# A decoder layer with two token mixers: where the first chunk of the gated attention is loaded and split

## The chip, the core and the metric

The kernel runs on one core of a Trainium2 chip. The core has TensorE (PE, matmuls), VectorE (DVE), ScalarE (ACT) and GpSimd (POOL) for arithmetic, and SyncE (SP), which here only issues transfers (DMAs) between the chip's main memory and the on-chip memory. ACT issues some transfers too. Each engine takes its instructions in the order in which they are written, and an instruction waits until the semaphores of what it needs have risen. The metric is the device time of one execution in microseconds.

## The reference

One step of a layer with `D_MODEL` = 1024, for a prompt of 2048 tokens and 8 sample tokens:

```
shift, scale, gate = c @ w_c + b_c
h = x * (1 + scale) + shift
z = h @ w_in + b_in        # q, k, v | attn gate | conv GLU in | conv gate | merge gates mA, mB
A: o = dilated sliding-window attention, three groups of heads, weighted by their softmax sums
   a = (o * silu(attn gate)) @ w_pa
B: u = GLU -> causal depthwise conv, width 31 -> LayerNorm -> swish
   b = (u * silu(conv gate)) @ w_pb
y = (sigmoid(mA) * a + sigmoid(mB) * b) @ w_o
x_out = LayerNorm(alpha * x + gate * y)
```

The outputs are `x_out` of prompt and samples, the new keys and values, and the tail of the convolution. All is float32.

## The kernel before, in words

Every large product is made of reduced-precision matmuls: each operand is split into a high part H (a copy rounded by ACT) and a low part L (the rest, subtracted by DVE or POOL), and PE adds up H·H, H·L and L·H. A split is therefore always two instructions, ACT first.

**The product z** (`quad`, L498) takes nearly 1800 us in two passes. Beside it, generators called lanes write the attention, the convolution and the combination of heads into the same instruction streams: `tick` (and, at the end, `run_lanes`) steps the lane that is due by an assumed clock, and a lane's `yield` tells how much later its next step is due. What a lane issues stands behind what was written before on each engine. The last pairs of z are the merge gates; they are evicted by ACT (L698, L705) and stored to `tm_d` and `tn_d` on ACT's queue. The gated attention goes to `og_d` (4 x 128 channels x 2056 tokens), the gated convolution to `cg_d`, both in main memory.

**The output's weights** are 16 pieces of 128 x 1024: pieces 0 to 3 are w_pa (tiles `wc0H`, `wc0L`), 4 to 7 w_pb (`wc1H`, `wc1L`), 8 to 15 w_o (`wc2`, `wc3`). `p_load` loads a piece into an `xr` buffer; there are three of them, in the pool "op". A buffer is taken again when its old content has been read, and the load waits for the last reader. `p_split` (L1439, L1440) splits piece x with ACT and with DVE (odd x below 8) or POOL (the others), and then issues the load of piece x + 3.

**The lane `early_out`**, which opens "op" when the attention is done, loads pieces 0 to 2 and splits pieces 0 to 3 beside the last pairs of z, one step every 4 us of the lanes' clock.

**The output stage** opens the pool "rc" after z. It works through the tokens in eight chunks `cc` of 256. For chunk 0 it loads `og_d` and `cg_d` (`oc_load`, into `ocr`), splits them into `oH`, `oL` and `bH`, `bL` (`oc_split`, L1609, L1610: DVE for oL, POOL for bL), splits pieces 4 to 7, and loads the merge gates (`mrg`). Then PE computes four blocks of a (`pab`, 48 matmuls of oH and oL with `wc0`), four of b (`py`, of bH and bL with `wc1`), and the same for the other four blocks (L1709); DVE weighs and adds them; the product with w_o follows (L1765). Later chunks are loaded and split while the chunk ahead is computed. All these loads are on SP, in this order: pieces 4, 5, 6, `og_d`, `cg_d`, piece 7, pieces 8 to 10, `mrg`.

Of the kernel before, what the change touches and what calls it, by code (L numbers as in the profile page):

```python
# [9 lines left out]
F32R = mybir.dt.float32r  # L10
AF = mybir.ActivationFunctionType
OP = mybir.AluOpType
# [4 lines left out]
P = 128  # L17
D = 1024
L = 2048
# [22 lines left out]
def f32(ap):  # L42
    return ap.bitcast(F32)
# [3 lines left out]
def hybrid_layer(ctx: ExitStack, tc: tile.TileContext, I, O):  # L47
    nc = tc.nc
    ctx.enter_context(tc.manual_schedule())
    PE, ACT, DVE, POOL = nc.tensor, nc.scalar, nc.vector, nc.gpsimd  # L50

    def ld(out, in_):
        nc.sync.dma_start(out, in_)
# [42 lines left out]
    def flush(every=True):  # L96
        fns = [x for x in post if every or x[0] <= clock["pe"]]
        post[:] = [x for x in post if x not in fns]
        for _, fn in fns:
            fn()  # L100
# [33 lines left out]
    og_d = dp.tile([4, P, T], F32, name="og_d")  # L134
# [1284 lines left out]
    pieces = []  # L1419
# [5 lines left out]
    def xbuf():  # L1425
        return op_[0].tile([P, D], F32, name="xr", tag="xr", bufs=3)

    def p_load(x):
        nm, kt, tag, k = pieces[x]
        praw[x] = xbuf()  # L1430
        ld(praw[x], I[nm][kt * P:(kt + 1) * P, :])

    def p_split(x):
        nm, kt, tag, k = pieces[x]
        if k == 0:
            wC[tag] = tuple((op_ if tag == 0 else rc_)[0].tile([P, 4, D], F32R, name=f"wc{tag}{n}") for n in "HL")
        H, Lo = (t[:, k, :] for t in wC[tag])
        r = praw.pop(x)
        ACT.activation(H, r, AF.Copy)  # L1439
        (DVE if k % 2 and x < 8 else POOL).tensor_tensor(Lo, r, f32(H), op=OP.subtract)  # L1440
        if x + 3 < len(pieces):
            p_load(x + 3)

    op_, rc_ = [], []

    def early_out():

        while ("at", 1) not in done:
            yield 1.0
        leave("cv1")  # L1450
        op_.append(enter("op"))
        for x in range(3):
            p_load(x)
        yield 8.0
        for x in range(4):
            p_split(x)
            yield 4.0


    zdone = set()  # L1460
# [17 lines left out]
    def enter(name):  # L1478
        cm, pool = opened(name, bufs=1, side="right")
        open_[name] = cm  # L1480
        return pool

    def leave(name):
        flush()
        closed(open_.pop(name))
# [30 lines left out]
    for p in range(2):  # L1516
        state["p"] = p
        cv = None
        for n, pair in enumerate(quads[p]):
            kind, a, b = pair[0]  # L1520
            ut = None
            if kind == "ua":
                if cv is None:
                    cv = enter(f"cv{p}")
                    if p == 0:
                        at_lane.add(at_first())
                        mix_lane.add(conv_samples(cv))
                        mix_lane.add(norm_samples(cv))
                        mix_lane.add(conv_norm(cv))
                        smp_lane.add(samples())  # L1530
                    else:
                        at_lane.add(at_second())
                        mix_lane.add(conv_norm(cv))
                        mix_lane.add(combine(cv))
                        mix_lane.add(early_out())
                if a >= 2:
                    while ("conv", p, a - 2) not in done:
                        conv_step()
                    if p:
                        guard(("urows", a - 2))  # L1540
                ut = cv.tile([P, 1054], F32, name="u", tag="u", bufs=2)
                if p == 0:
                    POOL.memset(ut[:, 0:30], 0.0)
                else:
                    POOL.tensor_copy(ut[:, 0:30], utail[:, a, :])
                evs = ev_glu(a, col_of(pair[0]), col_of(pair[1]), ut)
            else:
                evs = evs_of(pair)
# [40 lines left out]
    rc = enter("rc")  # L1589
    rc_.append(rc)  # L1590
    psC = ctx.enter_context(tc.tile_pool(name="psC", bufs=4, space=PSUM))
    bH, bL, oH, oL = (rc.tile([P, 4, 264], F32R, name=n) for n in ("bH", "bL", "oH", "oL"))
    yH, yL = (rc.tile([P, 8, 264], F32R, name=n) for n in ("yH", "yL"))
    gate, lng, lnb = (rc.tile([P, D], F32, name=n) for n in ("gate", "lng", "lnb"))

# [5 lines left out]
    def oc_load(cc, z):  # L1601
        t0, n = 256 * cc, 256 if cc < 7 else 264
        r = ocr[z] = rc.tile([P, 4, 264], F32, name="ocr", tag="ocr", bufs=2)
        ld(r[:, :, :n], (og_d, cg_d)[z][:].rearrange("j p t -> p j t")[:, :, t0:t0 + n])

    def oc_split(cc, z):
        n = 256 if cc < 7 else 264
        (H, Lo), r = ((oH, oL), (bH, bL))[z], ocr.pop(z)
        ACT.activation(H[:, :, :n], r[:, :, :n], AF.Copy)  # L1609
        (DVE, POOL)[z].tensor_tensor(Lo[:, :, :n], r[:, :, :n], f32(H[:, :, :n]), op=OP.subtract)  # L1610
# [7 lines left out]
            out.append(t)  # L1618
        return out

    oc_load(0, 0)
    oc_load(0, 1)
    oc_split(0, 0)
    oc_split(0, 1)
    for x in range(4, 8):
        p_split(x)
# [72 lines left out]
    for cc in range(8):  # L1699
        n = 256 if cc < 7 else 264  # L1700
        mgn = []
        for d in range(8):
# [30 lines left out]
            if cc == 0:  # L1733
                p_split(8 + d)
                if d == 7:
                    for t in range(3):
                        xr_load(t)
                    ld(gate, rows_bcast(gate_d[0], P))
                    ld(lng, rows_bcast(I["ln_g"], P))
                    ld(lnb, rows_bcast(I["ln_b"], P))  # L1740
# [84 lines left out]
```

## Time and profile before

| what | value |
|---|---|
| time, median of 3 runs | 2204.65 us (2203.07 to 2206.36) |
| the profiled execution's own time | 2208.26 us |
| its span, first to last instruction | 2206.4 us |
| share of the span busy: PE, DVE, ACT, POOL | 96%, 60%, 42%, 42% |
| mean granted clock of PE | 0.984 |
| last matmul group of z starts | 1795.49 us |
| first matmul of the output stage starts | 1800.73 us |

The profile is of one execution. Rows of a timeline give start, duration, engine, line of the kernel, operation and tiles (out<-in), and in brackets the idle time ahead of it with the instruction that ended it. The chain of waits goes back from the last instruction to what released it at each step. "SPq" and "ACTq" are the issuing of transfers on SP and ACT; "DMA" in the chain is a transfer on its way. Idle time of an engine costs something only where another one waits for it in the end.

### The profile page before, as it was taken

Reading aid. Unit: us, or ns where it says so; the run is one execution under the profiler, and the core shown is the slowest. Engines: PE = TensorE matmul, PEld = TensorE weight load, DVE = VectorE, ACT = ScalarE, POOL = GpSimd, SP = SyncE. Lnnn points to the kernel's source line nnn. Section 1 sums busy time; section 2 is a strip of 40 time slices with the busy share of each in tenths; the row PEclk is TensorE's granted clock in tenths of the full one; section 3 lists DMA queues with packets and bytes.
Section 4 is the critical chain, followed back from the end, with each engine's and each line's share of the span. In section 5 each row is a group of like instructions: output and inputs, shape, how many; then the busy total and the mean of one; then the engine's idle time right before and its main releaser. Section 6 shows DMA issues by size and latency. Waiting matters only on the chain.

```text
span 2206.4 us, 36413 instructions
## 1 busy us (share of the span) xinstructions
PE 2109.8 (96%) x13185; PEld 1864.7 (85%) x13185; DVE 1333.1 (60%) x2121; ACT 918.3 (42%) x2056; POOL 930.2 (42%) x950
## 2 busy tenths in 40 slices
PE   7799999999998899989999999999999988999998
PEld 3799999999998869968888888888878877888886
DVE  4667776777758733444776677634467827555456
ACT  3424444444444535644444444456555533111110
POOL 2455454444634432454444445445323446232332
PEclk9899999999999999989999999999999999999999
DMA  8365455455668765435555556567898866333220
GB/s 262 94 178 185 144 185 160 154 156 185 196 200 275 227 210 175 152 104 148 163 165 161 169 164 190 187 189 234 263 296 262 261 212 223 124 124 106 97 98 31
DMA packets 404046, 392.09 MB, mean 178 GB/s; under 512 B 26585, under 2 KB 331277, under 8 KB 402833
## 3 DMA queue, kind: packets, MB, share of 16 engines
q1 hardware_dynamic: 336277, 342.63, 50.3%
q10 hardware_dynamic: 67588, 47.13, 6.7%
q8 instruction: 104, 1.70, 0.3%
q14 instruction: 77, 0.63, 0.1%
HBM read 245.91 MB, written 144.29 MB: 177 GB/s over the span
## 4 chain that ended last, share of the span: by engine, by line
PE 53%; DVE 4%; DMA 2%; issue 1%; POOL 1%; ACT 1%; ACTq 0%; SPq 0%; POOLq 0%; DVEq 0%
PE ps_Z L498 9%; PE ps_W L498 9%; PE ps_X L498 9%; PE py L1765 8%; PE pab L1709 5%; PE ps_Y L498 4%; PE ps_S L1208 3%; PE ps_U L1248 1%; PE ps_S L1233 1%; DVE yL L76 1%; PE ps_S L653 1%; DVE xr L80 1%; PE ps_U L1246 1%; DVE st L1648 0%; DMA u<-orow 0%
## 5 line engine op out<-in xcount | busy, mean ns | idle before, releaser
L247 POOL TENSOR_TENSOR bop<-raw,bop 128x512 fp32r<-128x512 f32 x341 | 485.8, 1430 | 568.2 <-ACT bop L238 441.3
L498 PE MATMUL ps_W<-As,bop 128*128 128x258 f32 (+1 forms) x2448 | 437.7, 327 | 15.8 <-DVE zst L80 15.8
L498 PEld LDWEIGHTS ps_W<-As,bop 128*128 128x128 f32 x2448 | 360.5, 191 | 57.1 <-DVE zst L80 18.6
L80 DVE SCALAR_TENSOR_TENSOR y<-u,cwT,y 128x1024 f32<-128x1024 f32 x240 | 357.8, 1491 | 1.8
L238 ACT ACTIVATE bop<-raw 128x512 fp32r<-128x512 f32 x409 | 251.5, 624 | 76.8 <-DVE raw L76 26.4
L498 PE MATMUL ps_X<-As,bop 128*128 128x258 f32 (+1 forms) x1224 | 220.3, 327 | 11.3 <-ACT c L568 6.7
L498 PE MATMUL ps_Z<-As,bop 128*128 128x258 f32 (+1 forms) x1224 | 224.6, 330 | 2.4 <-ACT c L568 2.2
L498 PE MATMUL ps_X<-Aa,bop 128*128 128x258 f32 (+1 forms) x1224 | 219.8, 328 | 5.2 <-ACT bop L238 1.6
L498 PE MATMUL ps_Y<-Aa,bop 128*128 128x258 f32 (+1 forms) x1224 | 218.6, 326 | 0.0
L498 PE MATMUL ps_Z<-Aa,bop 128*128 128x258 f32 (+1 forms) x1224 | 217.9, 327 | 0.0
L498 PEld LDWEIGHTS ps_X<-As,bop 128*128 128x128 f32 x1224 | 179.7, 191 | 30.2 <-ACT c L568 6.9
L498 PEld LDWEIGHTS ps_X<-Aa,bop 128*128 128x128 f32 x1224 | 182.0, 192 | 26.5 <-ACT bop L238 2.8
L498 PEld LDWEIGHTS ps_Z<-As,bop 128*128 128x128 f32 x1224 | 180.1, 191 | 22.4 <-ACT c L568 2.6
L498 PEld LDWEIGHTS ps_Z<-Aa,bop 128*128 128x128 f32 x1224 | 181.9, 191 | 18.2 <-issue 0.8
L498 PEld LDWEIGHTS ps_Y<-Aa,bop 128*128 128x128 f32 x1224 | 179.3, 190 | 18.3 <-issue 1.8
L1225 ACT ACTIVATE X<-X,mz 128x128 f32<-128x128 f32 (+1 forms) x192 | 87.0, 455 | 168.3 <-DVE mz L84 162.4
L80 DVE SCALAR_TENSOR_TENSOR zst<-ps_W,bT,c 128x258 f32<-128x258 f32 (+1 forms) x102 | 58.4, 573 | 136.4 <-ACT c L589 133.1
L247 DVE TENSOR_TENSOR bop<-raw,bop 128x512 fp32r<-128x512 f32 x68 | 51.9, 763 | 94.4 <-ACT bop L238 90.9
L80 DVE SCALAR_TENSOR_TENSOR X<-ps_S,tabh 128x512 f32<-128x512 f32 (+1 forms) x80 | 52.5, 656 | 83.0 <-PE ps_S L1208 76.0
L1662 ACT ACTIVATE xr<-xr,lnm 128x1024 f32<-128x1024 f32 (+1 forms) x16 | 19.9, 1244 | 183.7 <-POOL lnm L1661 171.2
L80 DVE SCALAR_TENSOR_TENSOR zst<-ps_Y,bT,c 128x258 f32<-128x258 f32 (+1 forms) x90 | 51.4, 571 | 71.3 <-PE ps_Y L498 48.6
L1208 PE MATMUL ps_S<-ak,aq 128*128 128x256 f32 (+1 forms) x256 | 90.4, 484 | 0.3 <-DMA ak<-zk 0.3
(309 smaller groups left out, 3786.8 us busy)
## 6 DMA issues: line engine op xcount, KB each, us to landing
raw<-w_in SPq DMA_DIRECT2D x205, 256.0 KB
raw<-tw_d SPq DMA_DIRECT2D x136, 256.0 KB
tw_d<-raw SPq DMA_DIRECT2D x102, 256.0 KB
tw_d<-t SPq DMA_DIRECT2D x34, 256.0 KB
rawb<-w_in SPq DMA_DIRECT2D x33, 256.0 KB
wc<-w_c SPq DMA_DIRECT2D x16, 512.0 KB
aq<-zq SPq DMA_DIRECT2D x16, 512.0 KB
xr<-x_prompt SPq DMA_DIRECT2D x16, 512.0 KB
```

The costliest lines, as they stand in the source:

```text
L76: DVE.tensor_tensor(out, a, b, op=op)
L80: DVE.scalar_tensor_tensor(out, a, s, b, op0=op0, op1=op1)
L238: ACT.activation(t[:, 0], r, AF.Copy)
L247: eng.tensor_tensor(t[:, 1], r, f32(t[:, 0]), op=OP.subtract)
L498: PE.matmul(acc[:, :n], w[:, i, b, :], a[:, b, off:off + n], start=start and b == 0 and x == 0, stop=b == 3 and x == 2, skip_group_check=True)
L653: PE.transpose(pt[:, i * P:(i + 1) * P], t[:, i * P:(i + 1) * P], ident)
L1208: PE.matmul(S[:, s:s + w, :], q_of(b), k_of(b, w), start=True, stop=True)
L1225: ACT.activation(X[:, s:s + w, :], X[:, s:s + w, :], AF.Exp, bias=mz[:, n, 0:1], accum_out=mz[:, n, 1:2])
L1233: PE.transpose(pt[:, s, :], X[:, s, :], ident)
L1246: PE.matmul(U[:, n, :], Y[:, s, :], v_of(b, 1), start=True, stop=False)
L1709: PE.matmul(p[:, :n], a, b[:, kt, :n], start=i == 0, stop=i == 11)
L1765: PE.matmul(py[h], a[:, d, c0:c0 + P], w[:, h * 512:(h + 1) * 512], start=f, stop=l)
```

## The change

The lane `early_out` gets a fifth step. After the split of piece 3 it takes `oH` and `oL` from the pool "op" (they were in "rc"), takes an `xr` buffer, loads the first 256 tokens of `og_d` into it, yields 5 us of the lanes' clock, splits it with ACT and POOL, and then issues the load of piece 6, which the split of piece 3 used to issue. The output stage no longer loads and splits `og_d` for chunk 0; the later chunks use the same `oH` and `oL` as before.

```diff
         (DVE if k % 2 and x < 8 else POOL).tensor_tensor(Lo, r, f32(H), op=OP.subtract)
-        if x + 3 < len(pieces):
+        if x + 3 < len(pieces) and x != 3:
             p_load(x + 3)
 
+    oH_ = {}
@@ early_out
         for x in range(4):
             p_split(x)
             yield 4.0
+        flush()
+        for x in "HL":
+            oH_[x] = op_[0].tile([P, 4, 264], F32R, name="o" + x)
+        r = xbuf().rearrange("p (j n) -> p j n", j=4)
+        ld(r, og_d[:].rearrange("j p t -> p j t")[:, :, 0:256])
+        yield 5.0
+        ACT.activation(oH_["H"][:, :, :256], r, AF.Copy)
+        POOL.tensor_tensor(oH_["L"][:, :, :256], r, f32(oH_["H"][:, :, :256]), op=OP.subtract)
+        p_load(6)
@@ output stage
-    bH, bL, oH, oL = (rc.tile([P, 4, 264], F32R, name=n) for n in ("bH", "bL", "oH", "oL"))
+    bH, bL = (rc.tile([P, 4, 264], F32R, name=n) for n in ("bH", "bL"))
+    oH, oL = oH_["H"], oH_["L"]
...
-    oc_load(0, 0)
     oc_load(0, 1)
-    oc_split(0, 0)
     oc_split(0, 1)
```

The order of the instructions shows where this puts them. A row is a line of the kernel, an operation, its tiles (with numbers that tell buffers apart) and the engines or DMA semaphores that it waits for.

On SP, before, from the load of piece 5 to that of the first w_o piece (`xr` are weight pieces):

```order
L53 DMA xr_19243<-w_pb 128x1024 [waits DMAHW6_49,DMAHW5_49,Pool_49]
L53 DMA xr_19266<-w_pb 128x1024 [waits DMAHW7_49,DMAHW3_49,DVE_49]
L53 DMA ocr_19331<-og_d_122 128x4x256 [waits PE_49]
L53 DMA ocr_19333<-cg_d_123 128x4x256 [waits DMAHW4_49]
L53 DMA xr_19343<-w_pb 128x1024 [waits DMAHW5_49,Pool_49]
L53 DMA xr_19347<-w_o 128x1024 [waits DMAHW6_49,DVE_49]
```

Here piece 6 waits for DVE, and the two chunks follow it. In the changed kernel the same stretch of SP reads:

```order
L53 DMA xr_19243<-w_pb 128x1024 [waits DMAHW6_49,DMAHW5_49,Pool_49]
L53 DMA xr_19311<-og_d_122 128x4x256 [waits DMAHW7_49,DMAHW3_49,DVE_49]
L53 DMA xr_19315<-w_pb 128x1024 [waits DMAHW7_49,Pool_49]
L53 DMA ocr_19335<-cg_d_123 128x4x256 [waits DMAHW4_49,PE_49]
L53 DMA xr_19343<-w_pb 128x1024 [waits DMAHW5_49,Pool_49]
L53 DMA xr_19347<-w_o 128x1024 [waits DMAHW6_49,DVE_49]
```

The load of `og_d` stands ahead of piece 6 with the wait that piece 6 had; piece 6 waits for POOL; `cg_d` follows.

On POOL, the splits from piece 2 to piece 6, before:

```order
L1440 TENSOR_TENSOR wc0L_19178<-xr_19112,wc0H_19177 128x1024 [waits DMAHW5_49,Activation_49]
L1610 TENSOR_TENSOR bL_19323<-ocr_19333,bH_19322 128x4x256 [waits DMAHW4_49,Activation_49]
L1440 TENSOR_TENSOR wc1L_19340<-xr_19210,wc1H_19339 128x1024 [waits PE_49,Activation_49]
L1440 TENSOR_TENSOR wc1L_19340<-xr_19266,wc1H_19339 128x1024 [waits DMAHW7_49,Activation_49]
L1440 TENSOR_TENSOR wc2L_19477<-xr_19347,wc2H_19476 128x1024 [waits DMAHW6_49,PE_49,Activation_49]
```

These are piece 2, bL, pieces 4, 6 and 8. In the changed kernel:

```order
L1440 TENSOR_TENSOR wc0L_19178<-xr_19112,wc0H_19177 128x1024 [waits DMAHW5_49,Activation_49]
L1466 TENSOR_TENSOR oL_19310<-xr_19311,oH_19309 128x4x256 [waits DMAHW2_49,DMAHW7_49,DVE_49,Activation_49]
L1621 TENSOR_TENSOR bL_19329<-ocr_19335,bH_19328 128x4x256 [waits DMAHW4_49,Activation_49]
L1440 TENSOR_TENSOR wc1L_19340<-xr_19210,wc1H_19339 128x1024 [waits PE_49,Activation_49]
L1440 TENSOR_TENSOR wc1L_19340<-xr_19315,wc1H_19339 128x1024 [waits DMAHW3_49,Activation_49]
```

oL has come from DVE, ahead of bL.

On ACT of the changed kernel, from the last eviction of z (`zst`) on:

```order
L698 ACTIVATE zst_19306<-ps_Z_19137,hbT_131 128x512 [waits DMAHW2_49,PE_49]
L56 DMA tm_d_124<-zst_19306 128x512 [waits Activation_49]
L1465 ACTIVATE oH_19309<-xr_19311 128x4x256 [waits DMAHW7_49]
L1620 ACTIVATE bH_19328<-ocr_19335 128x4x256 [waits DMAHW4_49,Pool_49]
L1439 ACTIVATE wc1H_19339<-xr_19210 128x1024
L1439 ACTIVATE wc1H_19339<-xr_19243 128x1024 [waits DMAHW6_49]
```

oH has the place that it had before (there L1609, reading `ocr`).

## The prediction

> **What bounds the kernel now.** I read the busy shares first, then the chain of waits around the change (1767 to 1830 us), then the timeline of each engine there.
>
> ```profile
> span 2206.4 us, 36413 instructions
> PE 2109.8 (96%) x13185; PEld 1864.7 (85%) x13185; DVE 1333.1 (60%) x2121; ACT 918.3 (42%) x2056; POOL 930.2 (42%) x950
> ```
>
> TensorE (PE) is busy nearly all the time, so what a change around 1800 us is worth is what it does to the few places where PE stands still. The last product of z and the first product of the output meet there. PE's timeline (start, duration, and in brackets the idle time before and who ended it):
>
> ```profile
> 1795.49 2.95 PE L498 MATMUL ps_Z<-Aa,bop 128*128 128x512 f32 x12
> 1800.73 0.38 PE L1709 MATMUL pab<-oH,wc0H 128*128 128x256 f32 x1 [2.29 <-ACT oH L1609]
> 1801.99 0.45 PE L1709 MATMUL pab<-oL,wc0H 128*128 128x256 f32 x1 [0.88 <-DVE oL L1610]
> ...
> 1809.18 0.28 PE L1709 MATMUL py<-bH,wc1H 128*128 128x256 f32 x1
> ...
> 1812.34 0.56 PE L1709 MATMUL py<-bH,wc1H 128*128 128x256 f32 x1 [1.94 <-ACT wc1H L1439]
> ...
> 1813.60 0.58 PE L1709 MATMUL py<-bH,wc1L 128*128 128x256 f32 x1 [0.48 <-DVE wc1L L1440]
> ```
>
> PE loses about 3 us at oH/oL, then computes the 48 matmuls of `pab` (1801.99 to 1809.18), and stops again in `py` until the split of piece 7, the last of w_pb, is there at 1813.60. Which of the two stops sets the end? The chain of waits (start, duration, what) says the second, and that it hangs on cg_d, not on og_d:
>
> ```profile
> 1789.01 2.89 DVE wc0L L1440
> ...
> 1791.92 0.33 SPq L53
> 1792.25 0.05 issue
> 1792.30 0.43 SPq L53
> 1792.73 0.05 issue
> 1792.78 7.75 DMA ocr<-cg_d
> ...
> 1804.14 3.38 POOL wc1L L1440
> 1807.52 0.02 issue
> 1807.54 3.67 DMA xr<-w_pb
> 1811.21 0.02 issue
> 1811.24 1.06 ACT wc1H L1439
> 1812.30 0.02 issue
> 1812.32 1.24 DVE wc1L L1440
> ```
>
> To be read as: at 1791.9 DVE has split piece 3 and frees its `xr` buffer; SP then issues three loads one behind the other, piece 6 (1791.92), og_d (1792.30) and cg_d (1792.78). cg_d lands at 1792.78 + 7.75 = 1800.53. Then bH and bL are split, then POOL splits piece 4 until 1807.52, which frees the buffer for piece 7; piece 7 lands, is split by ACT and DVE until 1813.56, and PE goes on at 1813.60. From cg_d's landing to PE's restart it is 13.07 us, all of it a chain.
>
> **The change, part by part.** The rows of the order shown with the change carry this part. On SP, og_d has taken the place and the wait of piece 6 (DVE's split of piece 3). Piece 6 now waits for POOL: the three `xr` buffers hold pieces 4 and 5, both unsplit, and og_d, so the only buffer that can come free is og_d's, by POOL's oL. cg_d is queued behind piece 6. On POOL, oL stands ahead of bL. On ACT nothing moved: oH still stands behind the last eviction of z and its store, and the four `wc1H` still stand behind bH, so behind cg_d.
>
> *Step 1, the load of og_d.* Issued at 1791.92 and not 1792.30, and first of its group. That is worth nothing, since oH is held by ACT's own order:
>
> ```profile
> 1798.47 0.69 ACT L698 ACTIVATE zst<-ps_Z,hbT 128x512 f32<-128x512 f32 x1 [1.37 <-PE ps_Z L498]
> 1799.19 0.33 ACTq L56 DMA_DIRECT2D tm_d<-zst  x1
> 1799.62 1.06 ACT L1609 ACTIVATE oH<-ocr 128x1024 fp32r<-128x1024 f32 x1 [0.46 <-ACT zst L698]
> 1800.61 1.06 ACT L1609 ACTIVATE bH<-ocr 128x1024 fp32r<-128x1024 f32 x1
> ```
>
> Before, og_d had already landed when ACT came to it (its idle time was ended by zst, not by a DMA). So oH stays at 1799.62 to 1800.68, and PE's first `pab` matmul at 1800.73.
>
> *Step 2, oL on POOL.* DVE's oL, and on POOL the same shape as bL:
>
> ```profile
> 1800.71 1.23 DVE L1610 TENSOR_TENSOR oL<-ocr,oH 128x1024 fp32r<-128x1024 f32 x1 [4.27 <-ACT oH L1609]
> ...
> 1818.88 0.42 DVE L80 SCALAR_TENSOR_TENSOR ev<-mrg,pab 128x256 f32<-128x256 f32 x1 [5.33 <-DMA mrg<-tm_d]
> ```
>
> ```profile
> 1801.74 2.44 POOL L1610 TENSOR_TENSOR bL<-ocr,bH 128x1024 fp32r<-128x1024 f32 x1 [10.93 <-ACT bH L1609]
> ```
>
> oL ends at 1800.70 + 2.44 = 1803.14, not 1801.94: PE's second `pab` matmul comes 1.2 us later. That lies inside the wait in `py`, so it costs nothing by itself.
>
> *Step 3, piece 6 and cg_d.* Piece 6 is issued when oL is done, 1803.16 with a 0.02 us step, takes 0.33 us of SP, then 0.05 us, and cg_d's issue starts at 1803.54, where it was 1792.78: 10.76 us later. Its time to land is not 7.75 us any more, since fewer transfers are in flight. The nearest row is the first `mrg` load, which has the same size and shape (512 KB, 128x4x256) and also follows a weight piece by one issue:
>
> ```profile
> 1807.98 5.92 SPq L53 DMA_DIRECT2D xr<-w_o  x3
> 1814.00 0.39 SPq L53 DMA_DIRECT2D mrg<-tm_d  x1
> ```
>
> Issued at 1814.00 and awaited by DVE until 1818.88: 4.88 us. Bounds: 3.67 us (piece 7 with nothing ahead of it) and 7.75 us (as before). I take 4.88: cg_d lands at 1803.54 + 4.88 = 1808.42, where it was 1800.53. That is **7.89 us later** (6.7 and 10.8 at the bounds).
>
> *Step 4, what hangs on it.* bH starts with cg_d's landing before (1800.61) and after. Behind it the order on every engine is as it was: four `wc1H` on ACT, bL and pieces 4 and 6 on POOL, pieces 5 and 7 on DVE, piece 7's load behind the split of piece 4. Piece 6 lands before cg_d, so `wc1H` of piece 6 doesn't wait. So the 13.07 us stay, and PE restarts in `py` at 1808.42 + 13.07 = 1821.5. `pab` is over by about 1810.4 and no longer covers anything. A gain here could be that POOL's 3.38 us for piece 4 shrinks to the 2.44 us that bL of the same size took, by 0.9; I see no row that would change beside it, so I take none and keep it for the range.
>
> *Step 5, passing on.* The w_o pieces and the `mrg` loads stand on SP behind piece 7, as before, and all later loads behind these; DVE's 5.33 us of waiting for `mrg` moves along. Nothing behind 1813.6 depends on a clock of its own that could take the shift back. The early rows keep their order; DVE's split of piece 1 has a changed set of waits (now POOL in it). If that is POOL's split of piece 0, it may cost it 0.2 us around 1783.4, which ends well ahead of piece 3's split and changes nothing.
>
> The sum against the profiled execution: 0 + 0 + 7.9 + 0, so span 2206.4 + 7.9 = 2214.3 and its own time 2208.26 + 7.9 = 2216.2. That execution is 3.6 us above the median of the runs, 2204.65; the same shift on the median gives **2212.5 us**.
>
> **Weighing the clock.** The granted clock (the last three columns are clock, DMA share, GB/s) around the restart of `py`:
>
> ```profile
> 1814.00:1816.00 2.00, 2.00 (x11) 2.00 (x11) 0.00 (x0) 0.00 (x0) 0.00 (x0) 0.50 0.58 162
> ...
> 1820.00:1822.00 2.00, 2.00 (x19) 1.96 (x17) 1.14 (x3) 0.74 (x2) 0.00 (x0) 1.00 1.08 355
> ```
>
> After stops of 1.94 and 0.48 us PE already runs at half clock, 11 matmuls in 2 us against 19 later. So the kernel before pays the slow restart, and a longer stop adds nothing. [...]
>
> **Rivals.**
> - *A, the wait is not the new oL.* If piece 6's wait on POOL is long fulfilled, SP issues it and cg_d right behind og_d, and cg_d lands near 1800.5. Then only POOL's order costs: bL ends 1803.14 + 2.44 = 1805.58 instead of 1804.18, 1.4 us later, so 2206.0: not slower than can be told. It decides from the moment that POOL's wait points to anything ahead of 1800. For it: the listing names the engine only. Against: pieces 4 and 5 are unsplit then, so no other buffer can be overwritten.
> - *B, the stop gets shorter.* If oH were split in ACT's gap ahead of 1798.47, PE would start `pab` right behind z (1798.44). All four stops of the PE rows shown come to 2.29 + 0.88 + 1.94 + 0.48 = 5.6 us, so 2199.1 is the most that it could give. Against: ACT's order, and even with an early oH `py` waits for the chain from cg_d, which would have to come earlier as well.
> - *C, the restart costs clock as well.* If the longer stop keeps the clock low 4 us longer, 22 matmuls at the 1814 row's 2/11 us stand in place of the 1820 row's 2/19 us: 1.7 us, so 9.6 us in all and 2214.3. For it: the stop is five times as long. Against: the clock is at half already, and its rows show nothing lower to fall to.
> - *D, cg_d lands as slowly as before* (7.75 us): 10.8 us, 2215.4. Against: the stores of z and two other loads that shared the DMA engines then are gone.
>
> **How the numbers follow.** Forecast 70%; C 8% and D 6%; A 12%; B 4%. Medians of this kernel spread by about 3 us, and 0.2% (4.4 us) is about what a measurement can tell from no change. Forecast, C and D are all slower than that: 84%; A is within: 12%; B 4%. The range goes from 2207.5 (landing at 3.67 us and POOL's 0.9 us gained make 5.8 us, or 2210.4, less the spread of the runs; A's 2206.0 stays outside) to 2217.0 (D with that spread). The likeliest case's own range, from its bounds, is 2210.4 to 2214.3.
>
> **What would show it.** Right, if in the profile after: oH on ACT still starts near 1799.6; oL on POOL takes about 2.4 us; SP's row of piece 6 stands near 1803.2 in place of 1791.9, with cg_d behind it; the chain of waits runs through oL, piece 6 and cg_d; PE waits in `py` until about 1821.5. Wrong, if cg_d is issued near 1792.7 (A), oH starts before 1798.5 (B), or what is behind 1821 is shorter than in the profile before, so that some of the shift is taken back.

## The result, and the profile after

The changed kernel takes 2218.38 us (median of 4 runs, 2212.84 to 2220.47), the kernel before 2203.86 us beside it (4 runs, 2202.88 to 2206.36): a ratio of 1.0054, 95% interval 1.0042 to 1.0066. The change makes it slower, by about half a per cent. The profiled execution is the shortest of the four, 2212.84 us.

The head of its page:

```profile
span 2211.1 us, 36411 instructions
PE 2111.4 (95%) x13185; PEld 1865.5 (84%) x13185; DVE 1329.9 (60%) x2120; ACT 918.5 (42%) x2056; POOL 934.2 (42%) x951
```

PE does the same 13185 matmuls in nearly the same busy time (2109.8 us before). Of the 4.7 us by which this span is longer, 3.1 are PE standing still. ACT's timeline shows the end of z (start, duration, operation, and in brackets the idle time ahead):

```profile
1792.69 0.69 ACT L698 ACTIVATE zst<-ps_Z,hbT 128x512 f32<-128x512 f32 x1 [1.37 <-PE ps_Z L498]
...
1793.78 1.06 ACT L1465 ACTIVATE oH<-xr 128x1024 fp32r<-128x1024 f32 x1 [0.40 <-ACT zst L698]
...
1803.88 1.06 ACT L1620 ACTIVATE bH<-ocr 128x1024 fp32r<-128x1024 f32 x1 [9.04 <-DMA ocr<-cg_d]
```

oH stands right behind the last eviction of z, as before, and ACT then waits 9.04 us for `cg_d`, where before bH followed oH at once. But all of it starts 5.84 us earlier than in the profile before (oH at 1793.78, not 1799.62): z itself ended earlier in this execution. So spans and absolute times of two profiles can't be set against each other here. What can is a distance: from the start of oH to the matmul at which PE goes on in `py` once piece 7 is split. PE's timeline of the changed kernel:

```profile
1794.88 0.39 PE L1718 MATMUL pab<-oH,wc0H 128*128 128x256 f32 x1 [2.24 <-ACT oH L1465]
1797.30 0.58 PE L1718 MATMUL pab<-oL,wc0H 128*128 128x256 f32 x1 [2.03 <-POOL oL L1466]
...
1805.93 0.38 PE L1718 MATMUL py<-bH,wc1H 128*128 128x256 f32 x1 [0.46 <-ACT wc1H L1439]
1807.43 0.39 PE L1718 MATMUL py<-bL,wc1H 128*128 128x256 f32 x1 [1.12 <-POOL bL L1621]
1810.71 0.58 PE L1718 MATMUL py<-bH,wc1L 128*128 128x256 f32 x1 [2.89 <-POOL wc1L L1440]
...
1815.29 0.58 PE L1718 MATMUL py<-bH,wc1H 128*128 128x256 f32 x1 [1.68 <-ACT wc1H L1439]
1816.55 0.58 PE L1718 MATMUL py<-bH,wc1L 128*128 128x256 f32 x1 [0.47 <-DVE wc1L L1440]
```

The distance is 1816.55 − 1793.78 = 22.77 us, against 1813.60 − 1799.62 = 13.98 us before: **8.79 us more**. PE now stops for the operands of `py` one by one: `wc1H`, bL, the splits on POOL, piece 7. The chain of waits runs through the places that the change made:

```profile
1793.78 1.06 ACT oH L1465
...
1794.91 2.35 POOL oL L1466
...
1797.28 0.33 SPq L53
...
1797.70 6.09 DMA ocr<-cg_d
...
1807.33 3.34 POOL wc1L L1440
...
1810.68 3.47 DMA xr<-w_pb
```

oL on POOL ends at 1797.26; SP, which could not go past piece 6 until then, issues piece 6 at 1797.28 and `cg_d` behind it at 1797.70. From its landing (1803.79) on it is the old chain: bH, bL, piece 4 on POOL, piece 7's load and split.

The 8.79 us split exactly into three terms, measured from the start of oH. `cg_d` was issued 6.84 us ahead of it (1792.78) and is now issued 3.92 us behind it: +10.76. It lands in 6.09 us, not 7.75: −1.66. From landing to restart it takes 12.76 us (1816.55 − 1803.79), not 13.07: −0.31.

### The profile page after: what moved, and what is told of

It reads as the page before. It is cut to its first block, busy times and chain, and to the rows that moved or that the text cites. A ratio compares the mean times of both kernels' runs of the same rounds, so it can differ in the third digit from the quotient of the medians.

```text
span 2211.1 us, 36411 instructions
## 1 busy us (share of the span) xinstructions
PE 2111.4 (95%) x13185; PEld 1865.5 (84%) x13185; DVE 1329.9 (60%) x2120; ACT 918.5 (42%) x2056; POOL 934.2 (42%) x951
## 4 chain that ended last, share of the span: by engine, by line
PE 50%; DVE 4%; DMA 2%; POOL 2%; issue 2%; ACT 1%; SPq 0%; ACTq 0%; POOLq 0%; DVEq 0%
PE ps_Z L498 9%; PE ps_W L498 9%; PE ps_X L498 9%; PE py L1774 7%; PE pab L1718 5%; PE ps_Y L498 4%; PE ps_S L1208 3%; PE ps_U L1248 1%; PE ps_S L1233 1%; DVE yL L76 1%; PE ps_S L653 1%; DMA mrg<-tn_d 1%; DVE xr L80 1%; PE ps_U L1246 1%; DVE st L1657 0%
## 5 line engine op out<-in xcount | busy, mean ns | idle before, releaser
L1718 PE MATMUL pab<-oH,wc0H 128*128 128x256 f32 (+1 forms) x256 | 74.7, 292 | 19.1 <-DVE ev L80 16.8
```

What stands on the lines that cost most here:

```text
L1718: PE.matmul(p[:, :n], a, b[:, kt, :n], start=i == 0, stop=i == 11)
```

## The experiments

Each run is compared with the kernel before, run beside it on the same chip. "Distance" is always from the start of oH to PE's restart in `py` on the split of piece 7; F is from the start of z's last eviction (L698) to the first product with w_o, for kernels in which that restart doesn't exist any more. In the kernel before, that eviction starts at 1798.47 and PE's timeline has the product at

```profile
1835.48 0.63 PE L1765 MATMUL py<-wc2H,yH 128*128 128x512 f32 x2
```

so F is 37.01 us.

| kernel | oH starts | distance | F | ratio to before, 95% interval |
|---|---|---|---|---|
| before, the profile of the prediction | 1799.62 | 13.98 | 37.01 | |
| before, profiled again | 1794.85 | 13.99 | 37.23 | |
| changed | 1793.78 | 22.77 | 45.95 | 1.0054 (1.0042 to 1.0066) |
| changed, again | 1791.64 | 22.90 | 46.17 | 1.0044 (1.0028 to 1.0060) |
| oL on DVE | 1795.75 | 21.36 | 44.52 | 1.0029 (1.0018 to 1.0040) |
| `og_d` into oL's memory | 1798.60 | 15.16 | 38.34 | 1.0007 (0.9996 to 1.0017) |
| piece 6 behind `cg_d` | 1803.65 | 15.04 | 38.04 | 1.0012 (1.0001 to 1.0023) |
| `og_d` split inside z | 1786.95 | none | 36.34 | 1.0010 (1.0000 to 1.0021) |
| `cg_d` early instead | 1801.19 | none | 35.40 | 0.9990 (0.9980 to 1.0000) |
| and piece 7 early | 1791.56 | none | 34.23 | 0.9984 (0.9974 to 0.9994) |
| and `mrg` early | 1792.95 | none | 28.37 | 0.9951 (0.9935 to 0.9967) |

### Both kernels again

No edit. The question is whether the distance is a property of the kernel or of one execution.

> The changed kernel once more, unaltered. Measure used in all runs: the distance from the start of oH on ACT (right behind the last store of z) to PE's restart in py (first matmul that needs the low part of piece 7); it was 13.98 us before and 22.77 us with the change, 8.8 us more. Theory Q (og_d borrows a weight buffer, so piece 6 and cg_d queue behind oL on SP): the distance is 22 to 23.5 us again and the time 8 to 11 us above before; what the result had beyond that is the spread of z. Rival Z (the new tiles in the pool disturb the stage of z, or the tail behind the restart): the time is 12 to 15 us above before again, with the distance still near 22.8, and the rest of it stands in z or behind the restart in this profile as well.

> The kernel before once more, for a second profile. Distance from the start of oH to PE's restart in py 13.9 to 14.1 us again. Open: behind the restart the first profile has 392.8 us to the end, and the five others so far 394.3 to 395.4. If that is spread, this profile has 394 to 395.5; if the changed pool layout lengthens the tail, it has about 392.8 again. The start of oH (end of z) has stood anywhere from 1791.6 to 1803.7 in these profiles, whatever the kernel; this one may stand anywhere in it.

The changed kernel took 2216.13 us (8 runs) against 2206.85. Its timeline over all engines:

```profile
1791.64 1.06 ACT L1465 ACTIVATE oH<-xr 128x1024 fp32r<-128x1024 f32 x1 [0.40 <-ACT zst L698]
...
1814.54 0.58 PE L1718 MATMUL py<-bH,wc1L 128*128 128x256 f32 x1 [0.46 <-DVE wc1L L1440]
```

and that of the kernel before, profiled a second time:

```profile
1794.85 1.06 ACT L1609 ACTIVATE oH<-ocr 128x1024 fp32r<-128x1024 f32 x1 [0.46 <-ACT zst L698]
...
1808.84 0.58 PE L1709 MATMUL py<-bH,wc1L 128*128 128x256 f32 x1 [0.61 <-DVE wc1L L1440]
```

The distances repeat within 0.13 us (22.90, 13.99), while the start of oH moves by several us in both kernels. So 8.8 to 8.9 us is the price of the change at this place, and the time, 9.3 us apart by the medians, is near it: the 12 to 15 us of rival Z did not come again. The second profile of before also shows 393.9 us from the restart to the end, where the first had 392.8, so 1.1 of the up to 1.8 us by which this stretch is longer in the changed kernel (394.6, 394.3) lies within the spread of one kernel.

### oL on DVE

```diff
-        POOL.tensor_tensor(oH_["L"][:, :, :256], r, f32(oH_["H"][:, :, :256]), op=OP.subtract)
+        DVE.tensor_tensor(oH_["L"][:, :, :256], r, f32(oH_["H"][:, :, :256]), op=OP.subtract)
```

> The change with oL on DVE, where it was before. Theory Q: piece 6's load waits for oL, so it and cg_d go out 1.1 to 1.2 us earlier (1.23 us on DVE against 2.34 to 2.44 on POOL): distance about 21.6 us, time about 1 us below the changed kernel. Rival Z, or a theory in which POOL's order (oL ahead of bL) is the cost: distance 20.5 or less if POOL is what bL waits for; no change at all if neither matters.

2212.55 us, ratio 1.0029. Its timeline over all engines:

```profile
1795.75 1.06 ACT L1465 ACTIVATE oH<-xr 128x1024 fp32r<-128x1024 f32 x1 [0.40 <-ACT zst L698]
...
1798.09 0.33 SPq L53 DMA_DIRECT2D xr<-w_pb  x1
1798.51 0.39 SPq L53 DMA_DIRECT2D ocr<-cg_d  x1
...
1817.11 0.58 PE L1718 MATMUL py<-bH,wc1L 128*128 128x256 f32 x1 [0.47 <-DVE wc1L L1440]
```

`cg_d` is issued 2.76 us behind oH's start instead of 3.92, as a split of 1.2 us in place of 2.35 makes it, and the distance falls by 1.4 us to 21.36; the 0.25 us beside the 1.16 are a quicker landing of `cg_d`. The engine of oL is thus a small part of the cost; 7.4 us stay with oL on its old engine.

### `og_d` in a memory of its own

The chunk is loaded into the place of oL and split there, so that it borrows no `xr` buffer. Piece 6 is loaded by the split of piece 3 again, as before the change; oL stays on POOL.

```diff
-        if x + 3 < len(pieces) and x != 3:
+        if x + 3 < len(pieces):
             p_load(x + 3)
...
-        r = xbuf().rearrange("p (j n) -> p j n", j=4)
+        r = f32(oH_["L"][:, :, :256])
...
-        p_load(6)
```

> The change without the borrowed buffer: og_d is loaded into the memory of oL itself and split in place, piece 6 is loaded after the split of piece 3 as before; oH, oL stay in the pool of the first weights and oL stays on POOL. Theory Q: SP issues piece 6, og_d, cg_d one behind the other as before; only POOL's order is left, bL 1.2 to 1.4 us later: distance 15 to 15.5 us, time 1 to 2 us above before. Rival Z: the time stays 8 us or more above before, since the pool and its tiles are as in the change.

2206.83 us against 2206.85. Its timeline over all engines:

```profile
1791.39 0.38 SPq L53 DMA_DIRECT2D oL<-og_d  x1
1791.86 0.46 SPq L53 DMA_DIRECT2D ocr<-cg_d  x1
...
1798.60 1.06 ACT L1465 ACTIVATE oH<-oL 128x1024 fp32r<-128x1024 f32 x1 [0.40 <-ACT zst L698]
...
1802.05 2.37 POOL L1620 TENSOR_TENSOR bL<-ocr,bH 128x1024 fp32r<-128x1024 f32 x1
...
1813.76 0.39 PE L1717 MATMUL py<-bH,wc1L 128*128 128x256 f32 x1 [0.76 <-DVE wc1L L1440]
```

With nothing borrowed, `cg_d` is issued 6.74 us ahead of oH again, and 7.6 of the 8.8 us are gone (22.77 to 15.16). What stays over 13.98 is 1.2 us: bL now starts 3.45 us behind oH's start, not 2.12, since oL stands ahead of it on POOL. That is close to the 1.4 us that the prediction put beside rival A for POOL's order; no run took this rest away alone.

### Piece 6 behind `cg_d`

The buffer is borrowed as in the change, but the load of piece 6 is written behind that of `cg_d`.

```diff
@@ early_out
-        p_load(6)
@@ output stage
     oc_load(0, 1)
+    p_load(6)
     oc_split(0, 1)
```

> The change with one move: the load of piece 6 is written behind that of cg_d, so cg_d does not stand behind it on SP; piece 6 still waits for oL. Theory Q, as the prediction has it (cg_d is what hangs): cg_d lands at about the start of oH plus 0 to 2 us, piece 6 at oL's end plus 4 us, which is just when its split is due; distance 15 to 16.5 us, time 1 to 3 us above before. A variant in which the late piece 6 itself is what counts: distance stays near 19 us or more, time 5 us or more above before.

2209.02 us, ratio 1.0012. Its timeline over all engines:

```profile
1796.44 0.50 SPq L53 DMA_DIRECT2D ocr<-cg_d  x1
...
1803.65 1.06 ACT L1465 ACTIVATE oH<-xr 128x1024 fp32r<-128x1024 f32 x1 [0.40 <-ACT zst L698]
...
1807.18 5.99 SPq L53 DMA_DIRECT2D xr<-w_pb  x2
...
1818.69 0.39 PE L1718 MATMUL py<-bH,wc1L 128*128 128x256 f32 x1 [0.76 <-DVE wc1L L1440]
```

Piece 6 is issued 3.53 us behind oH's start, as late as in the changed kernel (3.50). The distance is 15.04 all the same. So the late piece 6 costs nothing; what costs is `cg_d` queued behind it on SP. Together with the run before this settles the cause: there `cg_d` stood behind piece 6 but piece 6 had no wait for oL, here piece 6 has the wait but `cg_d` does not stand behind it, and each gave back 7.6 to 7.7 us.

### `og_d` loaded and split inside z

Here the change gets all that an early `og_d` can give: loaded into oL's memory behind piece 3, split by ACT and DVE with piece 2, ahead of z's last evictions, with the loads of the weights as before.

```diff
         for x in range(4):
             p_split(x)
+            if x == 0:
+                ... (oH, oL from "op"; r = oL's memory; load og_d into r)
+            if x == 2:
+                ACT.activation(oH_["H"][:, :, :256], r, AF.Copy)
+                DVE.tensor_tensor(oH_["L"][:, :, :256], r, f32(oH_["H"][:, :, :256]), op=OP.subtract)
             yield 4.0
```

> og_d really early, without harm to SP's order: it is loaded into oL's memory behind piece 3 and split in place (ACT, DVE) with piece 2, so that pab can begin when z ends; piece 6 and cg_d are loaded as before. Theory Q: PE's first stop (2.29 and 0.88 us) goes, pab ends 3 us earlier, and PE then waits that much longer in py: restart in py 14.0 to 15.2 us behind the start of the last eviction of z on ACT (before: 15.13), the time 0 to 1.2 us below before. Rival O: the time falls by about 3 us.

2206.99 us against 2205.67, ratio 1.0010 (1.0000 to 1.0021). PE's timeline:

```profile
1798.23 0.39 PE L1718 MATMUL pab<-oH,wc0H 128*128 128x256 f32 x1 [0.78 <-ACT zst L698]
...
1810.51 0.58 PE L1718 MATMUL py<-bH,wc1H 128*128 128x256 f32 x1 [2.28 <-ACT wc1H L1439]
1811.77 0.58 PE L1718 MATMUL py<-bH,wc1L 128*128 128x256 f32 x1 [0.47 <-DVE wc1L L1440]
```

PE starts `pab` after 0.78 us instead of 2.29 and loses nothing at oL, but the wait in `py` takes that back: the restart comes 14.28 us after the start of z's last eviction (1797.49), where it was 15.13 (1798.47 to 1813.60). The stop at oH and oL was not what bound this place. A time 0 to 1.2 us below before was expected; the interval says 0 to 4.6 us above it, so no gain is to be measured.

### `cg_d` early instead of `og_d`

If `cg_d` is the load that counts, it is the one to be moved. From the kernel before: `cg_d` is loaded behind piece 2 into the memory of bL and split there with piece 1, and `og_d` stays where it was.

```diff
         for x in range(3):
             p_load(x)
+        r = f32(bH_["L"][:, :, :256])
+        ld(r, cg_d[:].rearrange("j p t -> p j t")[:, :, 0:256])
         yield 8.0
         for x in range(4):
             p_split(x)
+            if x == 1:
+                ACT.activation(bH_["H"][:, :, :256], r, AF.Copy)
+                DVE.tensor_tensor(bH_["L"][:, :, :256], r, f32(bH_["H"][:, :, :256]), op=OP.subtract)
@@ output stage
-    oc_load(0, 1)
-    oc_split(0, 1)
```

> From the kernel before: cg_d, not og_d, is loaded and split early. bH and bL stand in the pool of the first weights, the chunk of cg_d is loaded into bL's memory behind pieces 0 to 2 and split in place (ACT, DVE) with piece 1; og_d stays where it was. Theory Q (the chain from cg_d sets PE's restart): that chain is gone; ACT splits pieces 4 to 6 right behind oH, POOL begins with piece 4, piece 7 goes out some 5 us behind the start of oH, and the distance falls from 13.98 to 10.3 to 11.5 us, the time 1.5 to 4 us below before. Rival O (the wait for oH and oL at the start of pab is what sets the end): distance and time as before, since oH and oL don't move.

2203.82 us against 2205.67, ratio 0.9990. Once oL is there, PE runs through the 48 matmuls of `pab` and the 48 of `py` with no stop, and stops behind them. The restart that was expected 10.3 to 11.5 us behind oH doesn't exist, since PE comes to piece 7 just as its split ends, 10.4 us behind oH. DVE's timeline and then PE's:

```profile
1818.04 0.42 DVE L80 SCALAR_TENSOR_TENSOR ev<-mrg,pab 128x256 f32<-128x256 f32 x1 [6.45 <-DMA mrg<-tm_d]
```

```profile
1818.52 0.39 PE L1716 MATMUL pab<-oH,wc0H 128*128 128x256 f32 x1 [2.09 <-DVE ev L80]
```

The next wait has taken the place of the old one: with its four `pab` and four `py` blocks done, PE can't begin the second half until DVE has read the first, and DVE waits for `mrg`. Its load stands on SP behind pieces 7 to 10; piece 10 takes the buffer of piece 7, whose split ends at 1811.60, and `mrg` is issued at 1812.04. At the other end a little is lost: oH now waits 1.25 us for `og_d` and starts 1.93 us behind z's last eviction, where it was 1.15. F falls by 1.6 us, not by the whole stop.

### Piece 7 early as well

Piece 7 takes one of the two `ocr` buffers, which is free since `cg_d` doesn't use it, and is loaded behind `og_d`.

```diff
-        if x + 3 < len(pieces):
+        if x + 3 < len(pieces) and x != 4:
             p_load(x + 3)
@@ output stage
     oc_load(0, 0)
+    praw[7] = rc.tile([P, 4, 264], F32, name="ocr", tag="ocr", bufs=2).rearrange("p d n -> p (d n)")[:, :D]
+    ld(praw[7], I["w_pb"][3 * P:4 * P, :])
     oc_split(0, 0)
```

> As the one with cg_d early, and piece 7 is loaded right behind og_d into the chunk buffer that cg_d no longer needs, so it waits for no split. Theory Q: the next thing that holds py is gone too; wc1 is all split some 6 to 8 us behind the start of oH, pab ends at about 9.6, and PE goes from pab to py without a stop; the first py block of four ends some 16 us behind the start of oH (before: 20.9), the time 3 to 6 us below before. Rival O: as before, or only what the one with cg_d early gains.

2202.96 us against 2205.67, ratio 0.9984. F is 34.23, and the timeline over all engines shows why no less:

```profile
1796.14 3.65 SPq L53 DMA_DIRECT2D xr<-w_o  x3
...
1807.24 0.42 DVE L80 SCALAR_TENSOR_TENSOR ev<-mrg,pab 128x256 f32<-128x256 f32 x1 [6.73 <-DMA mrg<-tm_d]
```

`mrg` still waits on SP behind pieces 8 to 10. The first of these is issued when POOL has split piece 4, the last when POOL has split piece 6 (the split ends at 1799.43): the same mechanism some loads further on. `mrg` is issued at 1799.88. PE goes through `pab`, `py` and 12 matmuls more with next to no wait, and then stops for 1.46 us. The expected 3 to 6 us below before is 1.3 to 5.7 by the interval.

### `mrg` early as well

```diff
     oc_split(0, 0)
+    mg = m_load(0, 0)
     for x in range(4, 8):
         p_split(x)
-    mg = m_load(0, 0)
```

> As the one with cg_d early and piece 7 behind og_d, and the first two loads of the merge gates are written ahead of pieces 8 to 10 instead of behind them. In the profile without this move DVE waits 6.73 us for the first of them, while PE has both blocks done. Theory Q carried on (what sets the end is the last load that stands behind a buffer wait on SP): DVE's first weighing starts when PE is through the first py block, some 4 us earlier, and the first product with w_o starts 30 to 31.5 us behind the start of the last eviction of z (34.2 without the move, 37.0 and 37.2 in the two profiles of before); time 5.5 to 7.5 us below before. Against it: the split of the w_o pieces on ACT and POOL stands behind each weighing and could be what holds the product with w_o; then it starts at about 34 as before this move, and the time doesn't fall further.

2195.56 us (2192.14 to 2199.57) against 2207.17, ratio 0.9951 (0.9935 to 0.9967): faster than both kernels. F is 28.37, below the 30 to 31.5 that were expected. Its timeline over all engines:

```profile
1788.13 0.44 SPq L53 DMA_DIRECT2D mrg<-tm_d  x1
...
1791.04 0.69 ACT L698 ACTIVATE zst<-ps_Z,hbT 128x512 f32<-128x512 f32 x1 [1.37 <-PE ps_Z L498]
...
1801.84 0.41 DVE L80 SCALAR_TENSOR_TENSOR ev<-mrg,pab 128x256 f32<-128x256 f32 x1
...
1819.41 0.63 PE L1774 MATMUL py<-wc2H,yH 128*128 128x512 f32 x2
```

DVE reads `mrg` with no wait in front. The gain of F, 37.01 to 28.37, is 8.6 us; the ratio says 7.3 to 14.3 us of 2207, about 11, where 5.5 to 7.5 were expected; the 8.6 us lie inside the interval. The three moves were added one on the other, so what the move of `mrg` is worth alone is not shown.

## Why the prediction was right

The forecast was slower by 7.9 us through one chain. The chain is there, step by step, and the cost at this place is 8.8 us.

*Step 1, the earlier load of `og_d` is worth nothing: right.* oH starts right behind the eviction of z, as put. The time of 1799.6 was not met (1793.78), because z itself ended earlier; the order on ACT was what the step rested on, and it held. The run with `og_d` split inside z shows more: even an oH that is there ahead of z's end is worth nothing measurable.

*Step 2, oL on POOL costs nothing by itself: right for the changed kernel.* oL took 2.35 us (put at 2.44), and PE's later start behind it lies inside the wait of `py`. It is a part of the wait of step 3, which counted it, and moving it back to DVE gave 1.4 us. Where `cg_d` is not held up, in the two runs that free it, oL ahead of bL on POOL goes with 1.1 to 1.2 us.

*Step 3, piece 6 and `cg_d`: the mechanism right, one term mis-sized.* The issue of `cg_d` against oH moved by 10.76 us, which is the figure on record; to the hundredth that is luck, since oL was 0.09 us shorter and the small steps around it that much longer. The landing was not as put: it was put at 4.88 us from the first `mrg` load, with bounds 3.67 and 7.75, and took 6.09. That alone makes 1.2 us, so `cg_d` came 9.1 us later, not 7.89. In the same profile the `mrg` load, the row that the estimate came from, landed nearly as quickly as before (SP's and DVE's timelines):

```profile
1816.94 0.39 SPq L53 DMA_DIRECT2D mrg<-tm_d  x1
```

```profile
1822.07 0.42 DVE L80 SCALAR_TENSOR_TENSOR ev<-mrg,pab 128x256 f32<-128x256 f32 x1 [5.58 <-DMA mrg<-tm_d]
```

1822.07 − 1816.94 = 5.13 us. So the two loads of one shape don't land alike, 6.09 against 5.13. The last part of the landing of `cg_d` looks like this in the table by stretches (stretch, length, busy time of the five engines, and in the last three columns the clock, the mean busy share of the 16 DMA engines, and GB/s):

```profile
1802.00:1803.50 1.50, 1.50 (x12) 1.50 (x12) 0.00 (x0) 0.00 (x0) 0.00 (x0) 0.80 0.06 21
```

From 1798.5 to 1801.5 the share was 0.87 and 302 GB/s were moved; from 1802.0 on it is what one engine of 16 would show alone (1/16 = 0.06). In the second profile of the changed kernel and in the one with oL on DVE, bH starts 6.08 and 5.93 us behind the issue of `cg_d`, here 6.18. The `mrg` load has others right behind it, so no such tail can be seen there; why the tail is there is open.

*Step 4, the 13.07 us stay: right*, with 12.76 (−0.31). POOL's piece 4 took 3.34 us, so the 0.9 us that were kept for the range did not come; DVE's split of piece 5 still stands beside it, and the last section shows what that costs.

*Step 5, no gain or loss behind the restart: right within what can be seen.* From the restart to the end of the span it is 394.6 us in the changed kernel, 394.3 in its second profile, and 392.8 and 393.9 in the two of the kernel before.

*The total.* The sum gives 7.9 us where 8.8 were measured at this place. The ratio, on the 2204.65 us that the forecast started from, makes 2216.6 us (2213.9 to 2219.2): 4 us above the 2212.5 put down, and 0.4 us inside the range. The bare median of the four runs, 2218.4 us, lies above the range's 2217.0. The upper end was added up too low: the lower end takes 2.9 us of spread off its 2210.4, the upper end adds only 1.6 to D's 2215.4, and with the same spread it would be 2218.3. The likeliest case's own upper end, 2214.3, is C's sum; its bound of 7.75 us to land makes 2215.4. So the mechanism was met, and that the time lies inside the range as well is in part luck. The ratio's interval is 9.3 to 14.5 us here; that of the second measurement, with twice as many runs, is 6.2 to 13.2 us and holds the 8.9 us of its profile. What the first measurement has beyond 8.8 us has no place in the two traces, and its cause is not shown.

*The rivals.* A (the wait isn't the new oL) falls with one row: oL ends at 1797.26, piece 6 is issued at 1797.28. B (the stop gets shorter) falls with ACT's order, and in the run that gave oH early with the time too. D (7.75 us to land) was nearer than thought: 6.09 lies between the forecast and it. C (the longer stop costs clock as well) is answered by the granted clock. The table by stretches (engines' busy time, then clock, DMA share and GB/s) of the kernel before:

```profile
1802.00:1804.00 2.00, 2.00 (x10) 2.00 (x11) 0.41 (x1) 2.00 (x3) 2.00 (x1) 0.54 0.03 8
1804.00:1806.00 2.00, 2.00 (x13) 2.00 (x13) 1.26 (x1) 0.50 (x1) 2.00 (x2) 0.61 0.00 0
...
1812.00:1814.00 2.00, 1.17 (x4) 0.88 (x5) 1.23 (x1) 0.29 (x1) 0.00 (x0) 0.60 0.41 164
...
1818.00:1820.00 2.00, 2.00 (x15) 2.00 (x13) 0.42 (x1) 0.00 (x0) 0.00 (x0) 0.69 1.09 375
```

and of the changed one:

```profile
1794.00:1796.00 2.00, 0.39 (x1) 0.19 (x1) 0.00 (x0) 0.83 (x1) 1.09 (x1) 0.94 0.35 131
...
1802.00:1804.00 2.00, 2.00 (x16) 2.00 (x16) 0.00 (x0) 0.12 (x1) 0.00 (x0) 0.85 0.05 16
...
1808.00:1810.00 2.00, 0.00 (x0) 0.00 (x0) 0.46 (x1) 0.00 (x0) 2.00 (x1) 0.85 0.00 0
...
1818.00:1820.00 2.00, 2.00 (x12) 2.00 (x12) 0.00 (x0) 0.00 (x0) 0.00 (x0) 0.59 0.95 327
```

In the stretches beside these the clock is 1.00 or 0.50, so each of these rows holds one switch, whose moment follows from its mean: with 0.54, full clock for 0.16 of 2 us, so down at 1802.2. Before, the clock goes down at 1802.2, up at 1805.6, down at 1812.4, up at 1819.2. After the restart at 1813.60 PE runs 5.6 us at half clock. In the changed kernel it goes down at 1795.8, up at 1802.6, down at 1809.4, up at 1819.6, and after the restart at 1816.55 PE runs 3.1 us at half clock. In the second profiles of the two it is 5.8 and 4.0 us. The longer stop costs no clock behind the restart: much of the slow time now lies inside the stop. The 4 us more of low clock that C put in did not come: it is 2.5 and 1.8 us less. The prediction's reason, that the old stop had already brought the clock down, is what the rows show.

## What to carry to other kernels

A load that takes a buffer inherits the wait for that buffer's last reader, and on a queue that issues in order, as SP does here, so does every load written behind it (here `cg_d`, which went out 10.76 us later against oH): before a buffer is borrowed for an early load, look for what stands behind its next user in that queue, and what that one feeds. Move early the load that the chain of waits names, not the one whose consumer stops first; here it was `cg_d`, and then piece 7 and `mrg` behind it, and most of the gain (5.9 of the 8.6 us of F) came only when the last of the three was out of the queue. Where the work ahead of a place varies from execution to execution, compare distances between two rows of the same profile.

## What the runs showed of the hardware

*The clock's switches lie on a grid.* The moments above are 3.4, 6.8 and 6.8 us apart before, and 6.8, 6.8 and 10.2 us in the changed kernel: multiples of 3.4 us in both profiles. Rows of 0.2 us tell the first and the last of the kernel before to two decimals:

```profile
1802.00:1802.20 0.20, 0.20 (x1) 0.20 (x2) 0.00 (x0) 0.20 (x1) 0.20 (x1) 0.90 0.00 0
...
1819.20:1819.40 0.20, 0.20 (x3) 0.20 (x3) 0.10 (x1) 0.00 (x0) 0.00 (x0) 0.93 1.10 374
```

Down at 1802.16 and up at 1819.23 make 17.07 us, five steps of 3.41. The table by stretches of the kernel before, for the step that ends with the switch at 1812.40:

```profile
1808.99:1812.40 3.41, 1.47 (x13) 1.26 (x12) 0.08 (x1) 1.06 (x1) 0.88 (x1) 1.00 0.98 384
```

PE was busy for 1.47 of its 3.41 us, and the clock went down at its end. Cut along this grid, the two profiles around the place show the clock going down after steps with PE busy for 0.56, 0.69, 0.70 and 1.47 us and staying up after 1.87 us and more; from half it stayed down after 1.37, 1.65, 1.88 and 2.93 us and went up after 3.11 us and more. In these rows it is the busy share of a step that goes with the switch: the old stop of 1.94 us, from 1810.40 to 1812.34, lies in the step with 1.47 us. Whether there are fixed limits between these values was not measured.

*DVE and POOL take turns in these splits.* DVE's split of 128x1024 takes 1.23 us where POOL does nothing beside it, POOL's split of piece 6, with DVE idle, 2.35 to 2.40. In the kernel with `og_d` in a memory of its own POOL's bL ends at 1802.05 + 2.37 = 1804.42, with DVE's split of piece 5 begun beside it:

```profile
1802.62 2.87 DVE L1440 TENSOR_TENSOR wc1L<-xr,wc1H 128x1024 fp32r<-128x1024 f32 x1 [7.15 <-ACT wc1H L1439]
```

bL takes no longer for it, and DVE's split ends at 1805.49, 1.07 us behind bL, a little less than the 1.23 us that it takes alone. The kernel before shows the same: piece 3 on DVE (1789.01 to 1791.89) ends 1.08 us behind POOL's split of piece 2 (1790.81), and piece 5 (1803.59 to 1805.26) 1.08 us behind bL (1804.18). POOL's split of piece 4, begun while DVE still has piece 5 to do, takes 3.3 to 3.4 us, about 1 us more than piece 6 right behind it. So in these rows whichever began first is not slowed, and the other is held. Why it is held is not shown: no run set one alone against both.

*z ends at different times.* oH, which follows z's last eviction in all but the kernel that splits `og_d` inside z, started between 1791.6 and 1803.7 us in the profiles of kernels that are alike up to there but for a few loads and splits. That spread is larger than the effect of any one edit here.
